# Releasing S5 and attention four mask pairs earlier in a two-layer hybrid block

## The chip, the cores and the metric

One core of one Trainium2 chip. The metric is device time of one launch in microseconds (us). A change of 0.2% is 4.6 us. Engines are named as in the profile: PE (matmul), DVE (vector), ACT (scalar), POOL (GpSimd), SP (whose queue issues most DMAs).

## The reference

Two layers over 512 tokens of width 1024: 256 context tokens and 256 latent tokens. In a layer, a half-step SwiGLU feed-forward is followed by three token mixers on one normalised input, a gated merge with an output projection, and another half-step feed-forward. The last layer returns the latent tokens alone.

```python
def hybrid_mixer(h, hc, need_ctx_out, w_in, ...):
    proj = h @ w_in
    proj_c = hc @ (w_in if need_ctx_out else w_in[:, :CTX_STATE_COLS])
...
    y_s5, y_s5_c = s5_mixer(u_c, u_l, need_ctx_out, ...)
    y_att, y_att_c = gqa_mixer(q_c, k_c, v_c, q_l, k_l, v_l, q_norm_w, k_norm_w, need_ctx_out)
    y_rw, y_rw_c = rwkv7_mixer(f_c, f_l, need_ctx_out, ...)

    def merge(gate_pre, ys5, yatt, yrw):
        g_s5, g_att, g_rw = jnp.split(jax.nn.sigmoid(gate_pre), N_BRANCH, axis=-1)
        mixed = g_s5 * (ys5 @ w_br_s5) + g_att * (yatt @ w_br_att) + g_rw * (yrw @ w_br_rwkv)
        return mixed @ w_out
```

S5 is a bidirectional linear recurrence in 16 groups; attention has 8 query heads on 2 key/value heads with normalised queries and keys and rotary positions; RWKV-7 is a bidirectional recurrence with a 64 by 64 state for each of 4 heads.

## The kernel before

Every product of the model's weights is made as three products of rounded parts: a weight `w` is split into a high part (ACT, L927 in `wsplit`) and a low part (DVE or POOL, L928), the activations into `hhi` and `hlo`, and PE sums high by high, high by low and low by high (`mm3`, L943 to L945). So each 128x256 piece of a weight costs ACT and DVE one operation and PE six products in a row of the mixers. Weights come over SP's queue into a few rotating buffers.

The RWKV-7 mixer (`Rwkv`) works in chunks of 64 tokens, in two halves of the 512 tokens (`hf` 0 and 1), each in two directions (`d` 0 and 1), each direction in two pieces (`q` 0 and 1). `piece` (from L164) builds the decayed keys with DVE, ACT and POOL, lets PE make the in-chunk products `it` (L211), and multiplies them with triangular masks on DVE: `AM` (L216) and `ZL` (L217), once for each of two 64-row parts. The last of these, `s.lastz`, is the mask whose place the change concerns. `solve_a` inverts the 16x16 diagonal blocks with a chain of 30 DVE operations on all blocks at once (L243 and L244, tile `stmp`), with transfers `Ad`, `G`, `Sd` and `D` through device memory around it. `solve_b` extends the inverse to 64 rows with four rounds of small PE products (`pv`, `pS`, `pw`, `pT`, L260 to L284). `loop` carries the state over the chunks, each step in three hops from PE to DVE or ACT and back (L306, L326, L336).

S5 (`s5_main`) runs in steps over sets of groups and directions: PE makes `s5v`, DVE rotates it (`s5ra` L704, `s5rb` L705), POOL adds, DVE runs four scans (`s5w`, L711), DVE and POOL rotate back (`s5qb` L717, `s5S`), PE makes the output `s5y`. Attention (`Att`) loads keys and values of each half (`atqw`, L827, one buffer that the queries share, L845), splits the values into `atvh` (ACT) and `atvl` (DVE, L831), normalises keys and queries (`atss` L810, `atqnk` and `atqnq` L814), makes their high and low parts (`atkh`, `atkl` L841, `atqs` L855), scores `ats` (L868), their maximum `atm` (DVE, L870), exponentials `atP` and outputs `ato`.

While RWKV's pieces and solves run, PE also makes the projections: S5's input u, key/value (`pkv`) and q (`pq`, with the weight parts `ghq` and `glq`), and 24 gates (`pg`, with `ghpg` and `glpg`) whose tanh goes to device memory (`gd`) and comes back for the merge. In the merge each branch's product `pb` is multiplied with its gate on DVE (L1410, L1426), added on POOL (L1411, L1427), and split into `hhi` (ACT, L1429) and `hlo` (DVE, L1430) for the output product `po`. Gates of odd number have their low part made by POOL, the others by DVE.

The order of instructions on each engine is not written by hand: a scheduler lists them from the traced program with a model of their costs, priorities (`high_priority` for weight splits) and the edges it is given. `issue_after(x)` is such an edge: the instructions that the block traces on the engine of `x` are queued behind `x`; those on other engines are not held by it. In `mixers` it stands around S5 and attention both, which are traced together, and since a mask is a DVE instruction it holds their DVE work alone. Each engine executes its list in order.

```python
        with tc.tile_pool(name="s5",bufs=1) as sp, tc.tile_pool(name="att",bufs=1) as ap, tc.issue_after(rw.after):
```

Of the kernel before, what the change touches and what calls it, by code (L numbers as in the profile page):

```python
# [52 lines left out]
class Rwkv:  # L53
# [303 lines left out]
    def run(s,between):  # L357
        h0=s.head(0,0); h1=s.head(0,1); s.prep(h0)
        between()
        s.prep(h1); s.solve_a(0)  # L360
        h0=s.head(1,0); h1=s.head(1,1); s.piece(*h0[:2],0,h0[2][0],h0[3][0])
        with s.K.tc.issue_after(s.lasts):
            s.piece(*h0[:2],1,h0[2][1],h0[3][1])
            s.solve_b(0); s.prep(h1)
        s.after=s.lastz; s.solve_a(1)
        l0=s.loop(0); l1=s.loop(1)
        for _ in range(3): next(l0)
        s.solve_b(1); next(l0); Y0=s.Y if not s.last else None
        for _ in range(4): next(l1)
        if not s.last: s.finish(0,Y0)  # L370
        s.finish(1,s.Y)
# [1126 lines left out]
```

## Time and profile before

| | us |
|---|---|
| median of 3 runs (2278.97 to 2280.85) | 2280.64 |
| the profiled execution | 2285.45 |
| its span, first to last instruction | 2283.7 |
| PE busy in the span | 2198.0 (96%) |
| DVE, ACT, POOL busy | 1592.2, 959.8, 591.2 |

The profiled execution is one run; 1.75 us of it lie outside the span, and it took 4.81 us more than the median of the timed runs. The stretches read below lie in the first layer's mixers (from 544 us on) and in the second layer's (from 1812 to 2058 us). The granted clock is 0.969 of full speed in the mean.

### The profile page before, as it was taken

What the parts mean: (1) busy time and instruction counts of PE and PEld (TensorE: products, weight loads), DVE (VectorE), ACT (ScalarE), POOL (GpSimd) and SP (SyncE); (2) the same over time, 40 slices, a digit from 0 to 9 for tenths busy, and PEclk for the clock granted to TensorE, in tenths of its full rate; (3) what the DMA queues carried; (4) which work ended last, traced back from release to release, by engine and by line L of the source; (5) the groups of instructions that cost most, each with busy time, mean ns of one, the idle gap of its engine ahead of it and who ended that gap; (6) DMA issues with size and microseconds to landing.
All of it is one profiled execution on the core that took longest, in us unless ns stands there. A gap on an engine that the chain in (4) does not pass through costs nothing.

```text
span 2283.7 us, 40197 instructions
## 1 busy us (share of the span) xinstructions
PE 2198.0 (96%) x14562; PEld 1886.7 (83%) x14562; DVE 1592.2 (70%) x3189; ACT 959.8 (42%) x1980; POOL 591.2 (26%) x712
## 2 busy tenths in 40 slices
PE   8999999989999999999999999999999898998999
PEld 5878888867888988888888887788887787898999
DVE  4889699686877655787477587546556758876665
ACT  4332343443444543533233344334334444565554
POOL 0074362232534332000000007605023235440000
PEclk9999999998999999999999999999997769999999
DMA  7456666233435435465366355546412434556664
GB/s 284 132 167 225 194 200 220 91 101 106 114 111 169 159 108 168 166 197 184 104 196 192 92 168 170 181 153 221 139 56 74 142 107 128 170 181 207 177 190 129
DMA packets 219820, 358.17 MB, mean 157 GB/s; under 512 B 53731, under 2 KB 93283, under 8 KB 218469
## 3 DMA queue, kind: packets, MB, share of 16 engines
q1 hardware_dynamic: 217460, 354.85, 49.1%
q8 instruction: 114, 1.87, 0.3%
q10 hardware_dynamic: 2160, 0.76, 0.1%
q14 instruction: 86, 0.70, 0.1%
HBM read 316.70 MB, written 38.81 MB: 156 GB/s over the span
## 4 chain that ended last, share of the span: by engine, by line
PE 79%; DVE 9%; issue 3%; POOL 3%; DMA 3%; ACT 2%; SPq 1%; DVEq 0%; POOLq 0%; ACTq 0%
PE p L943 17%; PE p L944 17%; PE p L945 17%; PE pg L945 2%; PE pg L943 2%; PE pg L944 2%; PE it L211 1%; PE po L945 1%; PE po L943 1%; PE po L944 1%; PE pq L944 1%; DVE s5w L711 1%; PE pq L943 1%; PE s5y L728 1%; PE pf L943 1%
## 5 line engine op out<-in xcount | busy, mean ns | idle before, releaser
L938 ACT ACTIVATE wh<-wr 128x512 fp32r<-128x512 f32 (+1 forms) x568 | 349.4, 619 | 697.1 <-PE p L944 577.3
L939 DVE TENSOR_TENSOR wl<-wr,wh 128x512 fp32r<-128x512 f32 (+1 forms) x568 | 412.7, 730 | 263.8 <-ACT wh L938 236.8
L944 PE MATMUL p<-hlo,wh 128*128 128x512 f32 (+1 forms) x1440 | 518.8, 361 | 1.5 <-DVE hlo L1130 0.9
L945 PE MATMUL p<-hhi,wl 128*128 128x512 f32 (+1 forms) x1440 | 517.6, 360 | 0.0
L943 PE MATMUL p<-hhi,wh 128*128 128x512 f32 (+1 forms) x1440 | 514.1, 362 | 1.9 <-ACT hhi L1129 1.1
L944 PEld LDWEIGHTS p<-hlo,wh 128*128 128x128 f32 x1440 | 273.8, 190 | 44.1 <-DVE hlo L1130 1.8
L943 PEld LDWEIGHTS p<-hhi,wh 128*128 128x128 f32 x1440 | 271.9, 190 | 44.7 <-issue 2.2
L945 PEld LDWEIGHTS p<-hhi,wl 128*128 128x128 f32 x1440 | 273.7, 190 | 40.6 <-issue 0.6
L1013 DVE SCALAR_TENSOR_TENSOR s<-ad,cb 128x1024 f32<-128x1024 f32 x224 | 286.3, 1278 | 6.4 <-DMA ad<-w_ada 3.4
L943 PE MATMUL p<-ghi,wh 128*128 128x512 f32 (+1 forms) x704 | 248.3, 353 | 0.0
L944 PE MATMUL p<-glo,wh 128*128 128x512 f32 (+1 forms) x704 | 248.2, 353 | 0.0
L945 PE MATMUL p<-ghi,wl 128*128 128x512 f32 (+1 forms) x704 | 248.2, 353 | 0.0
L945 PE MATMUL pg<-hhi,glpg 128*128 128x256 f32 x512 | 153.9, 301 | 7.5 <-DVE glpg L928 5.7
L943 PE MATMUL pg<-hhi,ghpg 128*128 128x256 f32 x512 | 151.5, 296 | 0.0
L944 PEld LDWEIGHTS p<-glo,wh 128*128 128x128 f32 x704 | 133.0, 189 | 18.6 <-DVE glo L1162 0.5
L943 PEld LDWEIGHTS p<-ghi,wh 128*128 128x128 f32 x704 | 133.0, 189 | 18.4 <-issue 0.4
L945 PEld LDWEIGHTS p<-ghi,wl 128*128 128x128 f32 x704 | 133.0, 189 | 17.9
L944 PE MATMUL pg<-hlo,ghpg 128*128 128x256 f32 x512 | 147.6, 288 | 0.0
L927 ACT ACTIVATE ghpg<-wrpg 128x256 fp32r<-128x256 f32 x176 | 72.5, 414 | 121.4 <-PE pg L944 99.7
L1113 POOL TENSOR_TENSOR rsf<-msf,mhalf 128x2 f32<-128x2 f32 x5 | 3.6, 713 | 430.3 <-DVE msf L1112 430.3
L945 PEld LDWEIGHTS pg<-hhi,glpg 128*128 128x128 f32 x512 | 99.7, 195 | 15.2 <-DVE glpg L928 8.2
L928 POOL TENSOR_TENSOR glpg<-wrpg,ghpg 128x256 fp32r<-128x256 f32 x88 | 73.0, 831 | 136.6 <-ACT ghpg L927 119.2
(726 smaller groups left out, 4281.2 us busy)
## 6 DMA issues: line engine op xcount, KB each, us to landing
wr<-w SPq DMA_DIRECT2D x480, 256.0 KB
ad<-w_ada SPq DMA_DIRECT2D x128, 512.0 KB
wrpg<-w_g SPq DMA_DIRECT2D x96, 256.0 KB
wr<-w SPq DMA_DIRECT2D x64, 192.0 KB
s5tab<-s5tabd SPq DMA_DIRECT2D x16, 640.0 KB
s5tabd<-s5tb SPq DMA_DIRECT2D x16, 384.0 KB
wrpf<-w_f SPq DMA_DIRECT2D x24, 256.0 KB
gd<-gt SPq DMA_DIRECT2D x24, 256.0 KB
```

The costliest lines, as they stand in the source:

```text
L211: nc.tensor.matmul(pi[:,c,:],BK[R,c].rearrange("p j b -> p (j b)"),s.ZL[par][R,hf,dq,c,o],start=True,stop=True)
L711: V.tensor_tensor_scan(w[:,jj,c,1:129],m,a[:,jj,c,:],initial=0.0,op0=ALU.mult,op1=ALU.add)
L728: x=hv(St[d][:,jj,c]); nc.tensor.matmul(hv(py[:,jj]),CLs[d][:,c,jj,sl],x[:,:,::-1] if d else x,start=False,stop=(d==1 and c==1))
L927: K.nc.scalar.activation(hi,raw,AF.Copy)
L928: (K.nc.gpsimd if eng=='pool' else K.nc.vector).tensor_sub(lo,raw,hi.bitcast(F32))
L938: nc.scalar.activation(hi[:,0:n],raw,AF.Copy)
L939: (nc.gpsimd if eng=='pool' or i<=K.PW else nc.vector).tensor_sub(lo[:,0:n],raw,hi[:,0:n].bitcast(F32))
L943: nc.tensor.matmul(ps,lhi,rhi,start=start,stop=False)
L944: nc.tensor.matmul(ps,lhi,rlo,start=False,stop=False)
L945: return nc.tensor.matmul(ps,llo,rhi,start=False,stop=stop).ins
L1013: nc.vector.scalar_tensor_tensor(K.junk,raw,1.0,K.cb[:,v,:],op0=ALU.mult,op1=ALU.mult,accum_out=K.M[L][:,v,ct:ct+1])
L1113: nc.gpsimd.tensor_tensor(rs[:,r],ms[:,r],K.mhalf[:,0:2],op=ALU.pow)
```

## The change

`rw.after`, the instruction behind which the DVE work of S5 and attention is held, is taken from `s.lastz` before `solve_b(0)` and the preparation of the second half's second direction instead of after them. So it is the last mask of the second half's first direction (its second piece, second part) instead of that of its second direction: four products `it`, eight mask operations, earlier. The same is done in both layers.

```diff
@@ -361,8 +361,8 @@
         h0=s.head(1,0); h1=s.head(1,1); s.piece(*h0[:2],0,h0[2][0],h0[3][0])
         with s.K.tc.issue_after(s.lasts):
             s.piece(*h0[:2],1,h0[2][1],h0[3][1])
-            s.solve_b(0); s.prep(h1)
-        s.after=s.lastz; s.solve_a(1)
+            s.after=s.lastz; s.solve_b(0); s.prep(h1)
+        s.solve_a(1)
         l0=s.loop(0); l1=s.loop(1)
         for _ in range(3): next(l0)
         s.solve_b(1); next(l0); Y0=s.Y if not s.last else None
```

On DVE, first layer, behind the last mask of the second half's first direction (`it_5563`; + is what now stands there, a row without a sign stood there before too):

```order
 L217 TENSOR_TENSOR ZL_4033<-it_5563,c_mask_4007 64x512
+L789 CAST atvh_6723<-ones_72 128x4x64
+L790 CAST atvl_6724<-atz_6725 128x4x64
+L791 CAST atmh_6727<-atz_6725 128x128
 L928 TENSOR_TENSOR glq_4912<-wrq_4893,ghq_4911 128x256
+L792 CAST atmT_6728<-atz_6725 128x512
+L794 CAST atsel_6733<-c_sel_4011 128x2
+L749 TENSOR_SCALAR s5bg_7730<-s5bg_7730 128x2
 L198 TENSOR_TENSOR BK_5846<-T_5839,En_5836 64x512
 L199 TENSOR_TENSOR BK_5846<-T_5839,En_5836 64x512
+L831 TENSOR_TENSOR atvl_6724<-atqw_6780,atvh_6723 128x2x64 x2
+L810 TENSOR_REDUCE atss_6787<-atsqk_6786 128x4
```

Attention's constants and first values now stand among the `glq` of the q weights; before, all of them stood behind the masks of `it_5858`, the last of the second direction. A little further on the same engine, among the next `glq` (`atqw_6807` is the second key/value load):

```order
+L811 TENSOR_SCALAR atss_6787<-atss_6787 128x4
 L928 TENSOR_TENSOR glq_4946<-wrq_4927,ghq_4945 128x256
+L711 SCALAR_TENSOR_TENSOR s5w_6769<-s5m4m_6746,s5ra_6764 128x128 x2
 L928 TENSOR_TENSOR glq_4964<-wrq_4961,ghq_4963 128x256
+L711 SCALAR_TENSOR_TENSOR s5w_6769<-s5m4m_6746,s5ra_6764 128x128 x2
+L814 TENSOR_TENSOR atqnk_6793<-atqw_6780,atrs_6788 128x256
 L928 TENSOR_TENSOR glq_4980<-wrq_4961,ghq_4979 128x256
+L831 TENSOR_TENSOR atvl_6724<-atqw_6807,atvh_6723 128x2x64 x2
 L928 TENSOR_TENSOR glq_4998<-wrq_4995,ghq_4997 128x256
+L810 TENSOR_REDUCE atss_6814<-atsqk_6813 128x4
```

S5's first scans, the first normalised keys and the values of the second load now alternate with the `glq`. On SP's queue that second load (L827) moves from behind the first gate weights to ahead of the q weight `wrq_5071`, and the first query load (L845) and the second S5 table (L691) move ahead of the first transfer `Ad` of the second half's solve. On PE, at the end of the second layer's mixers (`pg115` is the last gate product, `pb14` a branch product of attention, `po10` the first output product), before:

```order
L945 MATMUL pg115_21302<-hhi_86,glpg1156_21338 128x256
L943 MATMUL pg115_21302<-hhi_86,ghpg1156_21337 128x256
L944 MATMUL pg115_21302<-hlo_87,ghpg1156_21337 128x256
L945 MATMUL pg115_21302<-hhi_86,glpg1156_21338 128x256
L944 MATMUL pb14_21447<-hlo_87,ae41_21442 128x256
L945 MATMUL pb14_21447<-hhi_86,ae41_21442 128x256
L943 MATMUL pb14_21447<-hhi_86,ae41_21442 128x256
L944 MATMUL pb14_21447<-hlo_87,ae41_21442 128x256
L945 MATMUL pb14_21447<-hhi_86,ae41_21442 128x256
L943 MATMUL pb15_21470<-hhi_86,ae51_21465 128x256
```

and of the change:

```order
L945 MATMUL pg115_21302<-hhi_86,glpg1156_21338 128x256
L943 MATMUL pg115_21302<-hhi_86,ghpg1156_21337 128x256
L944 MATMUL pg115_21302<-hlo_87,ghpg1156_21337 128x256
L945 MATMUL pg115_21302<-hhi_86,glpg1156_21338 128x256
L945 MATMUL po10_21551<-hhi_86,glpo100_21555 128x256
L943 MATMUL po10_21551<-hhi_86,ghpo100_21554 128x256
L944 MATMUL po10_21551<-hlo_87,ghpo100_21554 128x256
L945 MATMUL po10_21551<-hhi_86,glpo100_21555 128x256
L943 MATMUL po10_21551<-hhi_86,ghpo102_21564 128x256
L944 MATMUL po10_21551<-hlo_87,ghpo102_21564 128x256
```

The last gate product had 41 branch products behind it ahead of the first output product; now none is behind it, and 31 output products stand between it and the first that needs the last part of `hhi`. In the first layer's end the gate products that stand in a row, without another product between them, grow from 148 to 238.

## Rows read from the trace of the kernel before

**Rows 1.** The page: busy time by engine (part 1), and the chain (part 4).
```profile
PE 2198.0 (96%) x14562; PEld 1886.7 (83%) x14562; DVE 1592.2 (70%) x3189; ACT 959.8 (42%) x1980; POOL 591.2 (26%) x712
...
PE 79%; DVE 9%; issue 3%; POOL 3%; DMA 3%; ACT 2%; SPq 1%; DVEq 0%; POOLq 0%; ACTq 0%
```

**Rows 2.** Windows, first layer; columns: stretch, length, engines' busy us, PEclk, DMA share, GB/s.
```profile
544.00:576.00 32.00, 32.00 (x444) 28.07 (x443) 12.97 (x25) 10.48 (x21) 2.69 (x3) 1.00 0.29 88
576.00:584.00 8.00, 7.79 (x98) 7.32 (x98) 7.94 (x23) 4.34 (x10) 3.90 (x5) 1.00 0.51 96
584.00:592.00 8.00, 6.13 (x45) 5.18 (x45) 7.56 (x22) 2.25 (x6) 4.56 (x4) 0.79 0.72 216
592.00:624.00 32.00, 29.12 (x313) 26.29 (x311) 24.96 (x60) 16.00 (x41) 16.10 (x18) 1.00 0.36 105
624.00:628.00 4.00, 4.00 (x26) 3.71 (x28) 3.94 (x7) 0.59 (x1) 3.33 (x4) 0.59 0.31 93
```

**Rows 3.** Timeline of DVE, first layer; columns: start, duration, what ran [idle before <-releaser].
```profile
545.58 0.69 DVE L217 TENSOR_TENSOR ZL<-it,c_mask 64x512 f32<-64x512 f32 x1
...
555.16 0.43 DVE L928 TENSOR_TENSOR glq<-wrq,ghq 128x256 fp32r<-128x256 f32 x1 [1.81 <-ACT ghq L927]
...
575.66 0.68 DVE L217 TENSOR_TENSOR ZL<-it,c_mask 64x512 f32<-64x512 f32 x1
...
577.21 0.68 DVE L704 TENSOR_TENSOR s5ra<-s5v,s5tab 128x512 f32<-128x512 f32 x1
...
582.36 1.37 DVE L711 TENSOR_TENSOR_SCAN s5w<-s5m4m,s5ra 128x128 f32<-128x128 f32 x4
...
583.64 0.40 DVE L814 TENSOR_TENSOR atqnk<-atqw,atrs 128x256 f32<-128x256 f32 x1
...
585.55 0.94 DVE L928 TENSOR_TENSOR glpg<-wrpg,ghpg 128x256 fp32r<-128x256 f32 x1
```

**Rows 4.** Timeline of PE, first layer: its two long waits.
```profile
586.55 0.39 PE L945 MATMUL pg<-hhi,glpg 128*128 128x256 f32 x1 [1.86 <-DVE glpg L928]
...
623.90 0.39 PE L868 MATMUL ats<-atkh,atqs 128*128 128x256 f32 x1 [1.82 <-DVE atm L870]
```

**Rows 5.** Timeline of DVE, second layer: the last mask of each direction.
```profile
1818.62 0.68 DVE L217 TENSOR_TENSOR ZL<-it,c_mask 64x512 f32<-64x512 f32 x1
...
1856.05 0.68 DVE L217 TENSOR_TENSOR ZL<-it,c_mask 64x512 f32<-64x512 f32 x1
```

**Rows 6.** Windows, second layer.
```profile
1812.00:1860.00 48.00, 47.50 (x466) 39.28 (x465) 23.97 (x47) 12.62 (x27) 10.55 (x15) 0.50 0.31 90
1864.00:1872.00 8.00, 7.69 (x110) 6.62 (x110) 6.80 (x18) 5.65 (x17) 4.37 (x6) 1.00 0.61 202
1900.00:1920.00 20.00, 16.77 (x435) 14.71 (x436) 15.84 (x28) 8.58 (x18) 7.66 (x10) 0.91 0.46 146
```

**Rows 7.** Timeline, first layer: the second key/value load and its first reader.
```profile
584.07 0.34 SPq L827 DMA_DIRECT2D atqw<-kvd  x1
...
586.85 0.51 ACT L830 ACTIVATE atvh<-atqw 128x128 fp32r<-128x128 f32 x2 [1.16 <-DMA atqw<-kvd]
```

**Rows 8.** Waits of PE, 1862 to 2070: us in total, times, longest.
```profile
PE ats L868 <- DVE atm L870: 2.9, 2, 1.9
...
PE p L336 <- DVE XV L328: 1.6, 2, 0.8
...
PE pg L945 <- DVE glpg L928: 1.5, 4, 0.5
```

**Rows 9.** Timeline around the end of the second layer's mixers.
```profile
2048.65 0.28 PE L945 MATMUL pg<-hhi,glpg 128*128 128x256 f32 x1
...
2048.77 0.28 PE L944 MATMUL pb<-hlo,ae 128*128 128x256 f32 x1
...
2057.16 0.39 PE L945 MATMUL po<-hhi,glpo 128*128 128x256 f32 x1 [1.77 <-DVE glpo L928]
...
2057.36 0.41 DVE L1430 TENSOR_TENSOR hlo<-egZL,hhi 128x256 fp32r<-128x256 f32 x1
```

## Prediction

> **What bounds the kernel now.** I read four views in this order. The page first: PE is busy for 96% of the span and carries 79% of the chain that ended last, DVE 9% [rows 1]. So time is won only where PE stands idle or runs at its lower clock, and the next views look for those places. The windows of the first layer's mixers show two kinds of stretch. From 544 to 576 us PE is busy for all 32 us at a granted clock of 1.00 while DVE works 12.97 us of 32; from 576 to 592 us DVE works 15.5 of 16 us and PE loses 2.08 us to idleness, and the clock falls to 0.79 in the second half of that; from 592 to 624 us PE loses another 2.88 [rows 2]. DVE is slack first and full afterwards, and the work that fills it is the work that the change moves.
>
> The DVE timeline shows why. The masks of the first direction end at 546.27 us (545.58 and 0.69). After them DVE only makes the low parts `glq` of the q weights, each after 1.8 us of idleness. The last masks of the second direction end at 576.34, and only then, within a microsecond, do S5's first operations start: s5ra at 577.21, the scans s5w at 582.36, atqnk at 583.64, and behind them `glpg`, the low part of a gate weight, at 585.55 [rows 3]. PE's timeline has the price: its gate product stood 1.86 us for that `glpg`, and the scores `ats` stood 1.82 us for `atm` (the running maximum of the scores) at 623.90 [rows 4]. In the second layer the same two masks are 37 us apart (1818.62 and 1856.05) [rows 5]. PE there runs at 0.50 for the whole of 1812 to 1860, with 47.50 of 48 us busy, and at 1.00 from 1864 [rows 6] (the levels of 1.2 and 2.4 GHz).
>
> **The change part by part.** No instruction comes or goes. What moves is (a) DVE work of S5 and attention from behind the last mask to behind the first direction's masks, and with it (b) loads, and through the scheduler (c) the end of each layer's mixers. The sum is made against the profiled execution, 2285.45 us, which is 4.81 us (0.21%) above the median of 2280.64; I subtract that difference at the end.
>
> (a) First layer. Between 576.27 and 585.55 us the block costs about 9 us of DVE. Its cover in the new place is DVE's idle time from 544 to 576: 32.00 − 12.97 = 19.0 us [rows 2]. It fits, if it goes in small pieces: the order puts at most s5ra, its twin s5rb (of the same shape, taken at the same 0.68) and two masks (0.69 and 0.68 like the rows of 545.58 and 575.66), 2.7 us together, between two `glq`, against 1.8 us of idleness before each [rows 3], so one `glq` is about 0.9 us late, and I count +0.9. In the old place the `glpg` wait of 1.86 us goes whole, and so does the dip after it: 0.21 of 8 us, 1.7 us [rows 2, 4]. That is −3.6. The wait for `atm` at 623.90 (1.82) and its dip (0.41 of 4 us = 1.6) lie behind the second S5 group's scans, which also come earlier; but the attention score waits don't vanish, they move: I take half, −1.7. The rest of PE's idleness from 592 to 624 is 2.88 − 1.82 = 1.1 us [rows 2, 4]; it may go or stay, and I take half, −0.5.
>
> (b) The loads. The second key/value load, of the one buffer `atqw`, now waits in SP's queue ahead of a q weight load, and on DVE `atvl` of that load stands ahead of `glq_4998`, the sixth from the masks on. It can start when atqnk has read the buffer: in the trace atqnk ends at 584.04, the load is issued at 584.07, and ACT reads it at 586.85, 2.8 us later [rows 3, 7]. DVE has one `glq` (0.42) to do meanwhile, so it stands about 2.4 us plus the 0.5 us of `atvh`, and the next `glq` is late by that less the 1.8 us it idles anyway: +1.1. Bounds: 0, if the q weights are a buffer ahead, and 2.9. The tables of S5 and the first q load are moved ahead of gate weights too; the weights were issued before use with DMA queues half empty (the DMA share is 0.29 from 544 to 576 [rows 2]), so I cost that at nothing; without this cover it is one load, 2.8 us.
>
> Second layer. DVE's released work stands 37 us earlier, but PE there is the slow one, at half clock, and gains nothing while its queue is full. What can go are the later waits on DVE: 2.9 us for `atm` and 1.6 us for `XV` between 1862 and 2070 [rows 8]. As in the first layer, I take half: −2.2, and 0.9 for half the dip in 1900 to 1920 (0.09 of 20 us) [rows 6]: −3.1. The low clock of 1812 to 1860 I leave as it is: the waits that precede it, up to 1812, lie ahead of the first row of the change; its bounds are in the rivals. The Trainium skill, "TensorE: Matmul & The Clock Gate", Part 1, says that the throttle is the default state and that sustained activity releases it. By that rule the 48 us would have run at the full level and there would be 24 us less to lose here; the trace doesn't agree, since PE is busy for 47.50 of these 48 us and stays at 0.50 [rows 6].
>
> (c) The second layer's end. Before, the last gate product (2048.65) was followed by 41 attention branch products before the output products, and these hid the last gate's way: tanh, write and read of the gate through memory, product with the branch, sum, and `hlo`, which ends at 2057.77 [rows 9]. That is 9.1 us after that matmul. Now all branch products stand ahead of it, and 31 output products follow it until the first that needs the last `hhi`: at the 0.12 us between the rows of 2048.65 and 2048.77, 3.7 us. PE would stand about 5.4 us less the 0.5 by which `hhi` comes ahead of `hlo`, 4.9, where it stood 1.77 [rows 9]: +3.1. Bounds: +0.5, if the last gates run while PE still waits for something else, and +6, with a clock dip like the one of rows 2 behind it. In the first layer the order has 148 gate products in a row at the end and 238 afterwards; nothing is exposed there, and it also means that chains which end earlier there are worth nothing by themselves.
>
> The second layer's waits on the gates' low parts, 1.5 us [rows 8], have the cause of the first layer's `glpg` wait, DVE full with the released block: −1.5, or nothing.
>
> Sum: +0.9 − 3.6 − 1.7 − 0.5 + 1.1 − 3.1 + 3.1 − 1.5 = −5.3. 2285.45 − 5.3 = 2280.15, less 4.81: **2275.3 us** in runs like the ones timed. With every halved or bounded term at its better end (−0.9, −1.7, −0.5, −1.1, −3.1, −2.6) the sum is 9.9 lower, at its worse end (1.7, 0.5, 1.8, 3.1, 2.9, 1.5) 11.5 higher.
>
> **The rivals.** (A) The forecast, a small gain, 2270 to 2278 us. (B) No change: waits only move, since the filler at the first layer's end is 90 products longer and the second layer pays its exposed end. For it: PE is 96% busy. Against it: the 3.6 us at 584 to 592 have a named cause which the order takes away. Time: the sum without the halves I took in later stretches (1.7 + 0.5 + 2.2 + 0.9 = 5.3) is 0: 2280.6.
>
> (C) Slower, and by one mechanism: DVE's queue stands at the second key/value load's `atvl` while PE has only q products left, PE starves for as long as in rows 4 (1.8 us), and the clock falls as it did there, but in a stretch with nothing denser behind it, so that it stays low as it did from 1812 to 1860. It decides at a PE wait of about 1.8 us for that `glq` or the next; I reckon 1.1. For it: the second layer's identical stretch did stay at 0.50 for 48 us [rows 6]. Against: the first layer's stretch ran at 1.00 for all its 32 us with the same kinds of product [rows 2], and DVE has 19 us of slack there. If half of the 32 us runs at half clock, 8 us are lost, and with the stall of 1.8, 9.8; half of the 3.6 at 584 to 592, 1.8, is still gained: 2280.6 + 9.8 − 1.8 = 2288.6 us.
>
> (D) Faster by much: the second layer's clock comes back early. Before, it was back by 1864, a few us after S5 and attention were released at 1856.7 [rows 5, 6]; S5's and attention's products are now free up to 37 us earlier. Each us at half clock costs half a us: 48 us cost 24; if it came back 20 us sooner, 10 us are gained beyond (A): 2265 us. What speaks against it is that PE shows 47.50 of 48 us busy at 0.50 already [rows 6], so a fuller queue need not lift it.
>
> (E) That the change does nothing is excluded: the rows of the order move.
>
> **How the numbers follow.** A change of 0.2% is 4.6 us, about what a measurement of this kernel can tell from none: faster means under 2276.1, slower over 2285.2. (A) 0.42, three quarters of it under 2276.1; (B) 0.16, all within; (C) 0.26, its range 2285 to 2298; (D) 0.16. Faster: 0.32 + 0.16 = 0.48; same: 0.10 + 0.16 = 0.26; slower 0.26. The likeliest case alone spans 2270 to 2278; leaving out the lower half of (D) and the upper part of (C), the range is 2263 to 2290.
>
> **What would show it.** Right: s5ra soon after the first direction's masks (near 550 us), no `glpg` wait near 586 and clock 1.00 from 584 to 592; a PE wait of 4 to 6 us at the second layer's last output products; a DVE wait for the load `atqw`, about 2.5 us. Wrong: granted clock under 0.9 anywhere between 544 and 576 (C); 0.50 in the second layer ending before 1845 (D), or lasting beyond 1862; waits of 1.8 us for `glpg` and `atm` as many as before, at other times (B).

## The result: slower by 0.54%, and all of it in the second layer

The changed kernel took 2296.24 us (median of 5 runs, 2288.06 to 2303.11) against 2280.85 us (5 runs, 2278.97 to 2285.31) for the kernel before: a ratio of 1.0054, 95% interval 1.0029 to 1.0079 (the quotient of the two medians is 1.0067). The forecast was 2275.3 us, a gain, and the time lies above the range. The profiled execution of the changed kernel took 2293.17 us, with a span of 2291.4.

The page of the changed kernel, its busy line, answers to [rows 1]:

```profile
PE 2198.5 (96%) x14562; PEld 1886.0 (82%) x14562; DVE 1587.1 (69%) x3189; ACT 959.0 (42%) x1980; POOL 584.7 (26%) x712
```

The same instructions, and nearly the same busy times: nothing here tells where the time went (its chain breaks off early and tells nothing either). So I cut the span by rows that stand in both programs: the first layer's mixers from its first `hlo` after the first norm (L1130) to the first `hlo` of the feed-forward's norm, the second layer's from last to last. In each stretch I added up PE's idle times and the time at granted clock 0.50. I count a microsecond of idleness as one and a microsecond at half clock as half of one; the second is an estimate from the two levels, 0.50 and 1.00, and a coarse one (last section). "Again" is a second profile of the same kernel.

| kernel | layer 1: us | PE idle | at 0.50 | layer 2: us | PE idle | at 0.50 |
|---|---|---|---|---|---|---|
| before | 525.1 | 31.9 | 27.3 | 394.9 | 33.4 | 105.0 |
| before, again | 525.2 | 31.7 | 27.3 | 394.0 | 34.1 | 100.7 |
| changed | 523.0 | 29.7 | 30.7 | 409.5 | 41.9 | 109.2 |
| changed, again | 524.4 | 29.1 | 37.5 | 410.8 | 43.7 | 110.3 |

The first layer gains 2.1 us (0.8 in the second pair), the second loses 14.6 (16.8). The first layer's gain is no more than executions scatter by: e1, e8 and g3 below have the changed kernel's first layer row for row on PE, DVE, ACT and POOL, and it takes 525.2, 525.4 and 525.5 us in them. The three stretches outside agree within 4 us each; together they are 4.9 us shorter in the changed kernel's first profile. Of the 14.6, idleness of PE is 8.5 and lower clock 4.2 / 2 = 2.1; the rest, 4.0, stands in no row and is within the coarseness of this count. (What is left of the second layer after its idleness and half of its time at 0.50 is 309.0 us before and 313.0 in the changed kernel; over all kernels below it is 308 to 315.)

**The first layer.** Windows of the changed kernel, to be laid beside [rows 2] (same columns):

```profile
544.00:576.00 32.00, 32.00 (x394) 28.77 (x395) 24.07 (x50) 17.30 (x40) 13.17 (x14) 1.00 0.49 132
576.00:584.00 8.00, 8.00 (x84) 7.30 (x82) 6.86 (x25) 3.63 (x8) 0.00 (x0) 1.00 0.41 137
584.00:592.00 8.00, 6.16 (x70) 5.13 (x70) 7.82 (x20) 2.29 (x7) 6.13 (x7) 0.92 0.27 88
592.00:624.00 32.00, 32.00 (x323) 29.44 (x320) 22.05 (x45) 16.19 (x37) 12.83 (x14) 0.97 0.42 120
624.00:628.00 4.00, 3.59 (x140) 2.60 (x139) 3.94 (x8) 1.57 (x4) 2.34 (x3) 1.00 0.34 129
```

From 544 to 576 DVE now works 24.07 us where it worked 12.97, and PE is still busy for all 32 at 1.00: the released block does fit beside the q products. Some of it ran ahead of this window (its first operation starts at 536.77), and from 536 to 544 PE is idle for 0.60 us, where it was busy for all 8 before (at a lower clock, 0.57 against 1.00). The `glpg` wait at 586 is gone and 592 to 624 is full. But a wait of the same size stands at 590.36, and longer ones follow. PE's timeline of the changed kernel:

```profile
590.36 0.39 PE L868 MATMUL ats<-atkh,atqs 128*128 128x256 f32 x1 [1.84 <-DVE atm L870]
...
638.25 1.79 PE L274 MATMUL pw<-T,AM 32*32 32x32 f32 x64 [2.80 <-DVE T L269]
...
679.23 0.43 PE L945 MATMUL pg<-hhi,glpg 128*128 128x256 f32 x1 [2.61 <-DVE glpg L928]
```

The second key/value load is issued 38 us earlier than in [rows 7]. DVE stands for it at `atvl`; the timelines of SP's queue, ACT and DVE:

```profile
545.82 0.32 SPq L827 DMA_DIRECT2D atqw<-kvd  x1
...
548.41 0.51 ACT L830 ACTIVATE atvh<-atqw 128x128 fp32r<-128x128 f32 x2 [2.58 <-DMA atqw<-kvd]
...
548.75 0.49 DVE L831 TENSOR_TENSOR atvl<-atqw,atvh 128x128 fp32r<-128x128 f32 x2 [1.54 <-ACT atvh L830]
```

PE shows no idle time at all from 546 to 552, so this stall costs nothing.

**The second layer.** Waits of PE from 1690 to 2100 us (total, times, longest), to be laid beside [rows 8], which begin later. The kernel before:

```profile
PE pq L944 <- DVE glq L928: 2.4, 2, 1.4
...
PE pg L945 <- DVE glpg L928: 1.5, 4, 0.5
...
PE pkv L944 <- DVE glkv L928: 1.2, 1, 1.2
```

The changed kernel:

```profile
PE pg L945 <- DVE glpg L928: 6.3, 8, 1.9
PE pq L944 <- DVE glq L928: 5.1, 6, 1.7
PE pg L945 <- POOL glpg L928: 3.3, 6, 1.0
...
PE pkv L944 <- DVE glkv L928: 2.2, 2, 1.1
...
PE ats L868 <- DVE atm L870: 0.3, 1, 0.3
```

The scores' wait for `atm` went from 2.9 to 0.3 us, as the prediction had it. What came in its place are waits for low parts of weights: all idle time ahead of `pg` went from 1.9 to 11.0 us, ahead of `pq` from 2.6 to 5.6, ahead of `pkv` from 1.9 to 3.8. One instance, in DVE's timeline of the changed kernel, and the PE row that waits for it:

```profile
1952.52 0.91 DVE L928 TENSOR_TENSOR glpg<-wrpg,ghpg 128x256 fp32r<-128x256 f32 x1
1953.35 0.87 DVE L340 TENSOR_TENSOR XV<-p,Xe 64x256 f32<-64x256 f32 x2
1954.25 0.69 DVE L870 TENSOR_REDUCE atm<-ats 128x1 f32<-128x512 f32 x1
1954.95 1.37 DVE L711 TENSOR_TENSOR_SCAN s5w<-s5m4m,s5ra 128x128 f32<-128x128 f32 x4
1956.24 0.67 DVE L1309 TENSOR_TENSOR hlo<-aty,hhi 128x512 fp32r<-128x512 f32 x1
1956.83 0.68 DVE L870 TENSOR_REDUCE atm<-ats 128x1 f32<-128x512 f32 x1
1957.43 0.75 DVE L928 TENSOR_TENSOR glpg<-wrpg,ghpg 128x256 fp32r<-128x256 f32 x2
...
1957.90 0.39 PE L945 MATMUL pg<-hhi,glpg 128*128 128x256 f32 x1 [1.86 <-DVE glpg L928]
```

Between the end of one `glpg` (1953.43) and the start of the next stand 4.0 us of the RWKV loop, S5 and attention, all of them in DVE's one list, and PE has used up the weights that were ready. The end of the mixers, timeline of the changed kernel, answers to [rows 9]: the last gate's tanh, the last `hlo` and the longest wait of the output products.

```profile
2061.75 0.37 ACT L1345 ACTIVATE gt<-pg 128x256 f32<-128x256 f32 x1
...
2068.38 0.43 DVE L1430 TENSOR_TENSOR hlo<-egZL,hhi 128x256 fp32r<-128x256 f32 x1 [0.20 <-ACT hhi L1429]
...
2073.81 0.38 PE L945 MATMUL po<-hhi,glpo 128*128 128x256 f32 x1 [1.16 <-DVE glpo L928]
```

PE does not stand for the late gate; the waits of all output products are 2.8 us, where they were 3.2.

### The profile page after: what moved, and what is told of

The parts are those of the page before. It is cut to its first block, busy times and chain, and to the rows that moved or that the text cites. A ratio compares the mean times of both kernels' runs of the same rounds, so it can differ in the third digit from the quotient of the medians.

```text
span 2291.4 us, 40201 instructions
## 1 busy us (share of the span) xinstructions
PE 2198.5 (96%) x14562; PEld 1886.0 (82%) x14562; DVE 1587.1 (69%) x3189; ACT 959.0 (42%) x1980; POOL 584.7 (26%) x712
## 5 line engine op out<-in xcount | busy, mean ns | idle before, releaser
L943 PEld LDWEIGHTS pg<-hhi,ghpg 128*128 128x128 f32 x512 | 102.3, 200 | 9.4 <-ACT ghpg L927 3.9
```

Source lines behind the costliest of these rows:

```text
L943: nc.tensor.matmul(ps,lhi,rhi,start=start,stop=False)
```

## The experiments

What had to be told apart, by the names that the expectations use. **T1**: the loss is made in the second layer by the DVE work that its hold releases early. **T2**: both layers lose. **T3**: the loss is made by the second layer's new order of all its work, which the scheduler makes even where only the first layer's hold moves. **T4**: the early release in the first layer leaves something that the second pays for. Later came **T5**: the length of the second layer's stretch at half clock, which is the largest single sum in the table above, is decided by how the small products of the RWKV solves stand among the q products. S5's and attention's shares were open under each.

### One layer at a time

`e1_first_layer` releases early in the first layer alone:

```diff
-            s.solve_b(0); s.prep(h1)
-        s.after=s.lastz; s.solve_a(1)
+            s.after=s.lastz; s.solve_b(0); s.prep(h1)
+        s.after=s.lastz if s.last else s.after; s.solve_a(1)
```

> The early release in the first layer alone; the second layer keeps its old release. Theory T1 (all of the loss is made in the second layer's mixers, where the released DVE work crowds the weights' low parts and the second solve; the profiled runs put +14.6 us there and -2.1 in the first layer): 2277 to 2281 us, and an L1 stretch from its first norm to the next of 395 us as before. Theory T2 (both layers lose in most runs, the profiled one being a lucky one): 2285 to 2290.

Measured: 2293.79 us, ratio 1.0059 (1.0038 to 1.008). Both ranges were missed. Layer 1 took 525.2 us, layer 2 409.8: the whole loss again, and in the layer whose hold was not touched. T1 falls as the sole cause. The order shows why: 962 lines of PE's order in the second layer differ from before. Its waits are others than the change's, too; PE in the second layer of this kernel:

```profile
PE p L336 <- DVE XV L328: 3.8, 2, 2.0
PE pq L944 <- DVE glq L928: 3.5, 5, 1.1
...
PE ato L898 <- ACT atph L895: 2.7, 1, 2.7
PE po L943 <- ACT ghpo L927: 2.5, 3, 1.8
...
PE pg L945 <- DVE glpg L928: 1.5, 4, 0.5
```

The sum of idle time is the change's (41.7 to 41.9 us), but the waits for DVE's `glpg` are as short as before (all idle time ahead of `pg` is 4.1 us, where before has 1.9 and the changed kernel 11.0). So there isn't one wait that the release makes; the new order loses in many places.

`e2_second_layer` releases early in the second layer alone (`s.after=s.after if s.last else s.lastz` in the last of these lines).

> The early release in the second layer alone. T1: 2294 to 2300 us, the whole loss and the first layer's 2 us more, with the run-to-run scatter of the change (about 15 us). T2: 2285 to 2290.

Measured: 2298.49 us, ratio 1.007 (1.0049 to 1.0092), in T1's range. Layer 2 took 404.5 us with 43.4 of idleness. Its first layer took 529.5 us in this profile, 4.4 more than before with the same rows in the same order, so that part is scatter of the execution. Of the second layer's waits:

```profile
PE pg L945 <- DVE glpg L928: 9.5, 10, 2.1
```

Each half of the change alone costs as much as both together, so the two losses aren't terms of a sum: each is a new order of the second layer that is worse than the old one. T3 describes e1; for e2 release and order can't be told apart.

### S5 or attention

For these the with-line that holds both is replaced by a hold around each piece, of its own for S5 and for attention; `early` is the change's place, `late` that of before. The edit of `e3_l1_att_early` (second layer: attention early, S5 late):

```diff
-            s.solve_b(0); s.prep(h1)
-        s.after=s.lastz; s.solve_a(1)
+            s.early=s.lastz; s.solve_b(0); s.prep(h1)
+        s.late=s.after=s.lastz; s.solve_a(1)
...
-               (7 if last else 13,attention(Att(K,L,ap,last)))]
-            done=[0,0]
+               (7 if last else 13,attention(A))]
+            done=[0,0]; hold={14:rw.late,7 if last else 13:rw.early if last else rw.late}
...
-                if next(g[i][1],0)==0: g.pop(i); done.pop(i)
+                with tc.issue_after(hold[g[i][0]]): more=next(g[i][1],0)
+                if more==0: g.pop(i); done.pop(i)
```

> In the second layer alone, attention is released early and S5 late. If attention's share of the DVE work (casts, first keys, queries and the maxima) delays the second solve's chain: most of the loss, 2290 to 2298 us. If it is S5's share: 2280 to 2284.

Measured: 2288.45 us, ratio 1.0034 (1.0016 to 1.0052), between the two ranges expected; PE's idle time in layer 2 is 37.2 us, 3.8 more than before.

`e4_l1_s5_early` is the other way round (second layer: S5 early, attention late).

> In the second layer alone, S5 is released early and attention late, the reverse of the run before: 2280 to 2284 us if attention makes the loss, 2290 to 2298 if S5 does. If both together are needed (DVE full only with both), this and the run before each lose 3 to 6 us.

Measured: 2275.41 us, ratio 0.9978 (0.9963 to 0.9993): faster, which none of the three expectations had, though PE idles 4.2 us more. The idle times of e3 and e4 add up to e2's (3.8 + 4.2 against 10.0, within the 2 us by which repeats differ); what makes e4 faster is the clock. Its second layer has 71.7 us at 0.50 where before has 105.0, which is worth 16.7 us if each costs half; less the 4.2 that is 12.5, and the layer gains 6.1, so the half overstates here. That one long stretch was the thing to look at.

In the first layer, with a third place `mid`, behind the last mask of the second direction's first piece (h1 of the second half):

```diff
-            s.solve_b(0); s.prep(h1)
+            s.early=s.lastz; s.solve_b(0); s.piece(*h1[:2],0,h1[2][0],h1[3][0]); s.mid=s.lastz; s.piece(*h1[:2],1,h1[2][1],h1[3][1])
...
+            done=[0,0]; hold={True:(rw.late if last else rw.early),False:(rw.late if last else rw.late)}
```

This is `e5_l0_s5_early` (S5 early, attention late); `e6_l0_att_early_s5_mid`, `e7_l0_s5_early_att_mid` and `e8_l0_both_l1_s5` (both early in the first layer, S5 early in the second) differ in those two holds alone.

> First layer alone, S5 released behind the first direction's masks and attention behind the last mask as before. The second layer's order stays as before but for 43 lines of PE. Theory T3 (the first run's loss was made by the second layer's new order, which the scheduler makes even where only the first layer's hold moves): second layer 393 to 398 us, the whole 2277 to 2282 us. Theory T4 (an early release in the first layer leaves a state on the chip, queues or clock, that the second layer pays for): 2286 to 2294, with the second layer's stretch at 403 or more.

> First layer alone, attention released behind the first direction's masks and S5 behind the second direction's first piece; the second layer's order stays as before but for 43 lines of PE. T3: 2277 to 2283 us, second layer 393 to 398. T4: 2286 to 2294, second layer 403 or more.

> The mirror of the run before: first layer alone, S5 behind the first direction's masks and attention behind the second direction's first piece. Here the scheduler also makes another order of the second layer (1125 lines of PE differ, as many as in the change). T3 in its strong form (the second layer's old order is better than most others): 2286 to 2296 us, second layer 400 to 412. T3 in its weak form (orders scatter both ways): anything, and only the second layer's stretch moves. T4: as the run before.

> The change in the first layer; in the second layer S5 early and attention late. If S5's early release is itself what gained 6 us in the fourth run, and attention's what loses: 2272 to 2279 us, second layer 386 to 392. If the fourth run's gain belongs to its particular order: 2284 to 2296.

Measured, with the two layers and the length of the long stretch at 0.50 (it begins 102 to 117 us into the layer in every kernel; in the changed kernel it falls into four pieces, which add up to 54.6):

| kernel | us | ratio (95%) | layer 1 | layer 2 | PE idle, layer 2 | long stretch at 0.50 |
|---|---|---|---|---|---|---|
| before | | | 525.1 | 394.9 | 33.4 | 54.6 |
| e3 | 2288.45 | 1.0034 (1.0016 to 1.0052) | 525.4 | 396.2 | 37.2 | 54.6 |
| e4 | 2275.41 | 0.9978 (0.9963 to 0.9993) | 525.4 | 388.8 | 37.6 | 20.5 |
| e5 | 2265.36 | 0.9931 (0.9903 to 0.9958) | 518.1 | 380.1 | 35.0 | 20.5 |
| e6 | 2265.77 | 0.9925 (0.9903 to 0.9947) | 525.6 | 377.1 | 34.4 | 20.5 |
| e7 | 2268.41 | 0.994 (0.9915 to 0.9966) | 516.7 | 384.1 | 36.2 | 23.9 |
| e8 | 2280.75 | 0.9975 (0.995 to 1.0001) | 525.4 | 387.9 | 34.3 | 47.8 |

Three of these edits in the first layer make the kernel faster by 0.6 to 0.75%, mostly in the second layer, whose hold they leave alone. For e5 and e6 neither T3's range nor T4's held: both expected the second layer at 393 us or more, and it took 380.1 and 377.1. T2 had fallen already, since the first layer loses nothing in the changed kernel. In the first layer itself S5's early release is worth 4 to 9 us (e5, its repeat and g4 below, e7) as long as attention is not released at the same place; with both early (e8, e1) nothing of it is left, nor with attention early and S5 at `mid` (e6). e8 was to add the good halves, and missed: its long stretch is 47.8 us.

The windows show what the second layer gains. In the kernel before, the whole stretch at half clock:

```profile
1809.20:1863.80 54.60, 53.06 (x509) 44.26 (x508) 29.49 (x58) 14.75 (x31) 14.96 (x19) 0.50 0.32 87
```

In e5, the same 54.6 us from the fall of the clock on, in two pieces:

```profile
1796.90:1817.40 20.50, 18.92 (x180) 16.44 (x178) 16.33 (x29) 3.77 (x9) 8.41 (x12) 0.50 0.36 105
1817.40:1851.50 34.10, 31.43 (x486) 26.00 (x475) 24.28 (x61) 18.52 (x45) 14.42 (x17) 1.00 0.48 137
```

At 0.50 PE does 9 matmuls in a us, at 1.00 14 (of another mix). In the long stretch 34.1 us of half clock are missing, worth 17 us if each costs half, and the second layer is 14.8 us shorter with 1.6 us more idleness. (All of the layer's time at 0.50 falls from 105.0 to 63.1 us; at half each that would be 21, which is more than the layer gained.) The hold there was not touched; PE's order in it differs from before's in 43 lines. Up to 1814.39 in e5, 3 us before its clock rises, PE's rows in the second layer are those of the kernel before in the same order. A piece of the difference just ahead of the rise of e5's clock (- before, + e5; names are output <- inputs):

```
 L943 MATMUL pq_17867<-ghq_17892,hhi 128x256
-L260 MATMUL pv_18399<-T_18397,AM_16886 32x32 x16
+L260 MATMUL pv_18399<-T_18397,AM_16886 32x32 x14
 L944 MATMUL pq_17867<-glq_17893,hhi 128x256
...
 L943 MATMUL pq_17867<-ghq_17902,hhi 128x256
-L260 MATMUL pv_18399<-T_18397,AM_16886 32x32
 L944 MATMUL pq_17867<-glq_17903,hhi 128x256
...
-L260 MATMUL pv_18399<-T_18397,AM_16886 32x32 x11
+L260 MATMUL pv_18399<-T_18397,AM_16886 32x32 x12
 L943 MATMUL pq_17867<-ghq_17914,hhi 128x256
```

One small product of the solve no longer splits two groups of q products: 11 of them follow one another where 6 and 5 did. e1, e2, e3 and e8, with 47.8 to 54.6 us, have no such run of 11 there; e5, e6 and e7 have it, e4 has one a little further on, and the changed kernel, whose stretch is in pieces, has one of 12 behind the last `pv`. Such a run is not enough by itself: the kernel before has one of 12 at 1811.5, ahead of the first `pv`, and its clock stays at 0.50 until 1863.8; the repeat of the changed kernel (below) has its run of 12 at 1819.4 in a stretch that stays at 0.50 from 1813.6 to 1861.4.

### The clock or the order: the small products in blocks

`g1_before_blocks` is the kernel before with one edit in the second layer, which lets the scheduler issue the small products of that solve in long rows instead of a few between q products:

```diff
-            s.solve_b(0); s.prep(h1)
+            with (s.K.tc.high_priority(offset=1000) if s.last else nullcontext()): s.solve_b(0)
+            s.prep(h1)
```

`g3_change_blocks` is the same edit in the changed kernel, `g4_l0_s5_blocks` in e5. `g2_l0_att_mid` moves attention alone, in the first layer, to `mid`, with S5 late; PE's order in its second layer is that of before, row for row.

> The kernel before, with one thing else: in the second layer the first half's small solve products (pv, pS, pw, pT) get priority, so that PE does each kind in one block and 11 or 12 q products stand in a row between the blocks, where before they stand 1, 5 or 6 in a row. Theory T5 (how long the second layer stays at the lower clock is decided by how the small products are mixed with the q products right after it falls; the release's place acts on it only through the order): the low stretch that lasts 54.6 us in the trace before shrinks to 20 to 30, the whole 2262 to 2274 us. Theory T4 (the gain of runs 5 to 7 comes from the first layer's earlier release through some state): unchanged stretch, 2278 to 2286 us.

> First layer alone: attention behind the second direction's first piece, S5 behind the last mask as before. The second layer's order on PE is that of the kernel before, row for row. T5: the long stretch stays (50 us or more), 2274 to 2284 us, the difference to before being the first layer's own. T4: as runs 5 to 7, 2262 to 2272 us with a short stretch.

> The change, with the same priority for the second layer's small solve products as in g1. It sets the clock alike on both sides, so that its difference to g1 is what the early release itself costs or gains: if the extra waits for the weights' low parts (pg, pq: 8 us more than before in the change's trace) belong to the early release, 6 to 12 us slower than g1; if they too belong to the order of the small products, within 3 us of g1.

> The candidate: first layer with S5 released early and attention late (run 5), second layer as before but with the small solve products in blocks (g1). If the two gains are of different places (7 us of the first layer in run 5, the clock in the second): 2256 to 2266 us, under both kernels and under run 5. If they are the same gain: 2263 to 2268.

| kernel | us | ratio (95%) | layer 1 | layer 2 | PE idle, layer 2 | at 0.50, layer 2 |
|---|---|---|---|---|---|---|
| g1 | 2283.92 | 1.0017 (1.0004 to 1.0031) | 525.3 | 394.0 | 48.2 | 66.7 |
| g2 | 2281.31 | 0.9994 (0.9979 to 1.0009) | 527.6 | 394.5 | 34.2 | 100.8 |
| g3 | 2281.92 | 0.9999 (0.9982 to 1.0016) | 525.6 | 390.9 | 43.3 | 76.8 |
| g4 | 2264.21 | 0.9923 (0.9901 to 0.9944) | 515.7 | 381.3 | 37.2 | 71.4 |

g2: a hold of the first layer moved, the second layer's order unchanged, and the second layer takes 394.5 us with a long stretch of 54.6 as before. g2 moves attention alone, so S5's early release in the first layer needs other pairs, and the runs above have them. e5 and e6 differ in the first layer (518.1 and 525.6 us) and have the same second layer row for row on PE, DVE, ACT and POOL: it takes 380.1 and 377.1 us, each with a stretch of 20.5. The changed kernel, e1, e8 and g3 have the same first layer row for row and other second layers: these take 409.5, 409.8, 387.9 and 390.9. T4 falls: what the second layer takes goes with its own order and not with the first layer's release.

g1: less time at half clock (105.0 to 66.7 us, worth 19 us if each costs half; mean 0.78 in the window that was at 0.50), but 2283.92 us where T5 had expected 2262 to 2274:

```profile
1807.40:1862.00 54.60, 42.57 (x635) 37.51 (x637) 47.29 (x109) 21.00 (x51) 23.32 (x28) 0.78 0.39 110
```

PE gets through 635 matmuls where it did 509, but it idles 12 us of these 54.6, and the layer as a whole takes as long as before, with 14.8 us more idleness. PE's waits in g1's second layer (its line numbers are one higher):

```profile
PE pg L946 <- DVE glpg L929: 7.8, 8, 2.3
...
PE it L211 <- DVE BK L198: 3.0, 2, 2.5
PE vt L140 <- DVE AM L287: 2.8, 2, 2.4
...
PE pkv L945 <- DVE glkv L929: 2.3, 2, 1.2
```

So the clock that comes back is no gain here: PE waits for work, of DVE above all, that it did not wait for in the slower stretch. And g1 does not show that the blocks brought the clock back. Its windows around the rise, and the first block on PE:

```profile
1807.40:1814.20 6.80, 4.92 (x20) 4.38 (x21) 6.66 (x11) 1.92 (x4) 4.10 (x6) 0.50 0.36 119
1814.20:1817.80 3.60, 2.90 (x30) 2.46 (x32) 3.57 (x9) 0.00 (x0) 2.21 (x4) 1.00 0.34 103
...
1817.72 1.29 PE L260 MATMUL pv<-T,AM 16*32 16x32 f32 x128
```

The clock is at 1.00 from 1814.20, ahead of the first block at 1817.72, and up to there the rows of PE, DVE, ACT and POOL in this layer stand in the order of the kernel before, which stays at 0.50 at that place. What differs is when they ran: PE waited about 1.1, 0.7 and 0.6 us more at 1789.6, 1791.9 and 1808.8. The case for T5 is e5 against before, and it is as strong as its repeats: three executions of one order of the second layer (e5, its repeat and e6) have 20.5 us, three of the other (before, its repeat and g2) 54.6.

g3 against the change: 2296.24 to 2281.92, with 109.2 to 76.8 us at 0.50. With the same blocks, before (g1) and change (g3) are within 2 us of each other: with an order that the blocks force, the early release costs nothing that can be measured. g4 is e5 with blocks, 2264.21 us; no different from e5's 2265.36, and in both of its expected ranges, so that it tells nothing between them.

### The same kernels once more

A second profile of the kernel before, the changed one and e5, without an edit, for what repeats.

> The kernel before once more, for a second profiled execution of the same program. If the order decides how long the second layer stays at the lower clock: the stretch from 112 us after that layer's last norm row lasts 45 us or more again, and PE waits 31 to 36 us in the layer. If it is chance of the execution: 20 to 30 us is as likely.

> The change once more. If its loss is of its order: PE waits 39 to 45 us in the second layer, of them 8 or more for gate weights' low parts, and the layer's low stretches again make 95 us or more. If the first profile was an unlucky one: waits of 33 to 37, or low stretches under 80.

> The kernel of run 5 once more. If the order decides: the low stretch is again 20 to 27 us and the second layer 377 to 386 us. If chance: 45 us or more is as likely.

2283.27, 2299.26 and 2264.27 us. Layer 2 took 394.0, 410.8 and 380.5 us (394.9, 409.5 and 380.1 the first time). The long stretch at 0.50 was 54.6 us again in the first and 20.5 again in the third; in the changed kernel 6.8 and 47.8 instead of four pieces. The accounting by layer stands on more than one execution.

## Why the prediction was wrong

- **The step that failed: "The second layer's waits on the gates' low parts, 1.5 us, have the cause of the first layer's `glpg` wait ... −1.5, or nothing."** The waits ahead of `pg` grew by 9.1 us, and those for the low parts of q and key/value weights, which were no term at all, by 3.0 and 1.9. I had carried over from the first layer that DVE is full only because the block is held back. In the second layer the low parts share DVE with the loop of the RWKV chains, S5 and attention wherever these stand, and once these were put among each other, `glpg` stood behind 4.0 us of them.
- **The premise under it:** the sum priced the rows that I saw move and took the rest of the second layer as it was. e1 shows that the second layer is put in another order by an edit in the first alone (962 lines of PE), and that this order loses the same 15 us, with other waits. So a sum over the moved rows could not have found the loss. A little of the growth lies ahead of that layer's release, where the release can't have made it: up to the first direction's last mask (1818.6 before, 1811.7 changed) PE idles 14.5 us before and 15.1 changed, with 1.9 us more ahead of `pkv`. The other 7.9 of the 8.5 us lie behind it.
- **A reading: the mask at 545.58 is not the last of the first direction but the first of the second.** A direction has four `ZL` masks, and the first direction's last one is, before and changed:

```profile
540.19 0.68 DVE L217 TENSOR_TENSOR ZL<-it,c_mask 64x512 f32<-64x512 f32 x1
...
536.16 0.68 DVE L217 TENSOR_TENSOR ZL<-it,c_mask 64x512 f32<-64x512 f32 x1
536.77 0.43 DVE L789 CAST atvh<-ones 128x256 fp32r<-128x256 f32 x1
```

  So the release comes 5.4 us earlier than the prediction took it. No term of the sum changes by it, but the cover was read over the wrong stretch. Nor does DVE make `glq` alone from 546 to 576: masks, copies and the transpose of the solve stand there too, and the idle time before a `glq` lies between 0 and 2.3 us.
- **First layer, −3.8 us by the terms: −2.1 and −0.8 measured, and nothing that can be told from none** (e1, e8 and g3 with the same rows). The cover of 19 us was there (DVE 24.07 of 32, clock 1.00), and the `glpg` wait went. The half that I left for "waits move" was too small: 1.84, 2.80 and 2.61 us stand at other rows. e5 and e7 show what there was to gain: S5's part of the release is worth 4 to 9 us, and with attention's it is gone.
- **The second key/value load, +1.1: nothing.** DVE stood 1.54 us, not 2.9, and PE did not notice.
- **`atm` and `XV` in the second layer, −2.2: right in sign and short in size.** `ats` went from 2.9 to 0.3 us, and the loop's `p` from 5.6 to 4.1. The dip of 1900 to 1920, −0.9, did not go: before has 3.4 us at 0.50 from 1908.2, the changed kernel 6.8 from 1918.5.
- **The exposed end, +3.1: nothing.** The last gate's way is 7 us (2061.75 to 2068.81) and is hidden by output products; they wait 2.8 us, not 3.2.
- **"The low clock of 1812 to 1860 I leave as it is."** True for the change (109.2 us against 105.0), but it was the largest sum at stake: the same layer has a long stretch of 20.5 us instead of 54.6 in e5, whose order there differs by 43 lines. Rival (D) had the stake and the wrong lever: with both released early (e2) the stretch lasts 51.2 us, with neither released early in that layer 54.6 (before) or 20.5 (e5). The prediction set the Trainium skill's rule on sustained activity ("TensorE: Matmul & The Clock Gate", Part 1) beside [rows 6]; the rows of before and e5 above disagree with it as those did: the clock is 1.00 where PE is busy for 31.43 of 34.10 us, and 0.50 where it was busy for 53.06 of 54.60.
- **Rival (C)** had the sign and a time near the result, but by a mechanism that did not happen: no PE wait at the second load, and clock 1.00 from 544 to 576.

What stays open: which rows of the new order make the waits one by one (e1 and the change lose the same time at different ones); what of e2's loss is release and what order; and the 4 us that stand in no row. That the long stretch goes with the second layer's order is shown by e5, its repeat and e6 against before, its repeat and g2. What about the order decides it is not shown, and the order is not all: g1's clock came back where before's did not, behind the same rows.

The fastest versions, e5, e6 and g4, beat both kernels: 2265.36, 2265.77 and 2264.21 us, 0.7 to 0.8% under the kernel before, 1.3 to 1.4% under the changed one by the medians. e5 and g4 hold attention where it was and release S5 of the first layer early; e6 does it nearly the other way round (attention early, S5 at `mid`) and is as fast, by the second layer's order alone.

## What to carry to other kernels

Where a scheduler writes the order, compare the whole order that an edit makes, the stages that the edit doesn't touch too, before pricing the rows it moves; here the loss lay in one that e1 did not edit. The stage at half clock was the largest sum at stake here: where there is one, compare the orders in which it is short and long, take a second profile of each, and count as a price the waits that come with the faster clock (g1). When work is released earlier on an engine that also prepares the next weights, price the wait for those weights first.

## What the runs showed of the hardware

PE stayed at half clock (1.2 GHz) for 54.6 us while it was busy for 53.06 of them, and came back to 2.4 GHz after 20.5 us in an order that differs by 43 lines. That length repeats between executions of these two: 54.6 and 54.6 us in before, 20.5 and 20.5 in e5, although runs of one kernel lie up to 23 us apart (e5). The same 54.6 us came in e3 and g2. It does not always repeat: the changed kernel had four pieces of 6.8 to 27.3 us in one execution, 6.8 and 47.8 in the other. That the clock in the records is real shows in like products of PE that follow each other, in before at 0.50 and in e5 at 1.00:

```profile
1827.07 0.41 PE L945 MATMUL pq<-ghq,hlo 128*128 128x256 f32 x1
1827.29 0.41 PE L943 MATMUL pq<-ghq,hhi 128*128 128x256 f32 x1
...
1818.21 0.28 PE L945 MATMUL pq<-ghq,hlo 128*128 128x256 f32 x1
1818.33 0.27 PE L943 MATMUL pq<-ghq,hhi 128*128 128x256 f32 x1
```

They start 0.22 us apart at 0.50 and 0.12 at 1.00. By these rows a microsecond at half clock costs 0.45, a little less than the half that is counted above.

In e1 the clock stayed low for as long, with PE as full and fewer matmuls in the same time (454, before 509); its window:

```profile
1809.90:1864.50 54.60, 53.14 (x454) 43.07 (x454) 21.48 (x48) 15.61 (x34) 9.26 (x11) 0.50 0.27 74
```

So neither how full PE is nor how busy DVE is (21.48 us of DVE here, 29.49 before, 16.33 + 24.28 in e5) would have told me in advance when the clock returns.
